# Layer 0: the FFN gate's adaLN projection moves from TensorE (attention) to VectorE (up projection)

## The chip, the cores and the metric

One Trainium2 chip (trn2), one core. The metric is device microseconds of one execution; lower is better. The kernel before was run three times: 1411.06, 1406.48 and 1403.56 us, median 1406.48 us.

## The reference, cut to what matters

Two layers of a decoder trunk on 512 tokens of width 1024, all in float32. In each layer six modulation rows of 1024 come from one product of the condition vector with `w_ada`; two of them, `g1` and `g2`, are gates on the output of the mixer and of the FFN:

```
cond = jax.nn.silu(c)
for l in range(DEPTH):
    mod = cond @ w_ada[l] + b_ada[l]
    sh1, sc1, g1, sh2, sc2, g2 = [m[:, None, :] for m in jnp.split(mod, 6, axis=-1)]
    h = x * (1 + sc1) + sh1
    y = hybrid_mixer(h, ...)                     # gMLP, retention, sparse attention, w_out
    x = layer_norm(DN_ALPHA * x + g1 * y, ln1_g[l], ln1_b[l])
    h = x * (1 + sc2) + sh2
    y = conv_ffn(h, w_up[l], conv_w[l], conv_b[l], w_down[l])
    x = layer_norm(DN_ALPHA * x + g2 * y, ln2_g[l], ln2_b[l])
```

So `g1` (columns 2048 to 3071 of `w_ada`) is needed after the output projection, and `g2` (columns 5120 to 6143) only after the down projection.

## The kernel before

**Stages.** Each layer runs its projections, then an attention stage, the output projection `w_out`, the up projection with its convolution, and the down projection. Large float32 products are split into three matmuls of a high and a low part (`mm3`, L449 to L451); ScalarE makes the high part of each weight tile (L125, `whi`) and VectorE, or GpSimd for the retention weights and `w_out`, the low part (L127, `wlo`). `Weights` (L92 to L160) walks one list of jobs in program order: loads go to SP's queue into three `wraw` buffers, and two jobs ahead are split into three `whi` and three `wlo` buffers.

**Where `w_ada` is multiplied.** `ADA_RUNS` puts the six rows into three banks of two runs of 1024 columns; bank 2 holds the gates, run 0 `g1` and run 1 `g2`.
- Layer 0, banks 1 and 2, are done by TensorE in the attention stage (`ada_bank`, L318): for each of 8 k and each run, one raw 512 KB tile is loaded through the job list and two matmuls (L327) multiply it, each giving 32 columns of the array to 512 columns of output. Here such a pair is called a group; each bank has 16. The profile records each of these float32 matmuls twice, so that a group is x4 in a row.
- Layer 1, all three banks, are done ahead by VectorE during layer 0's up projection (`ada_dve`, L332): each run loads eight 512 KB tiles on GpSimd's queue (L341) into four `araw` buffers and sums them into one `acc` tile (L343 once, then L345 seven times); then TensorE adds the 128 partitions up with matmuls by ones (L349, one group for each run), VectorE adds the bias (`ada_finish`, L363).

**Order of the work.** A scheduler sets the order within each engine from the program's order. In the attention stage `attention()` steps beside `filler()`: at each event of attention one step of the retention mixer (projections, then four chunks with L906, L917, L926, L932, L935) and, in `ADA_AT` steps, one group of L327. In the up projection, a loop over 22 column tiles `ct`, each `ct` is followed by three steps of `ada_ahead`. A step is one load and one accumulation, or the closing matmuls, or the bias.

**The gate's row.** `gate_row` (L1144) broadcasts a gate from `modg` into a `grow` tile with eight small DMAs on SP's queue (L1150). For the FFN it is called ahead of the `ct` loop.

Of the kernel before, what the change touches and what calls it, by code (L numbers as in the profile page):

```python
# [10 lines left out]
F32 = mybir.dt.float32  # L11
# [3 lines left out]
OP = mybir.AluOpType  # L15
AX = mybir.AxisListType

P = 128
# [3 lines left out]
KD = D // P  # L22
# [126 lines left out]
def tile_trunk(ctx, tc, I, tab, out, layers=L):  # L149
    nc = tc.nc  # L150
    V, A, G, T = nc.vector, nc.scalar, nc.gpsimd, nc.tensor
# [12 lines left out]
    def m4(name):  # L164
        return pool.tile([P, 1024], F32, tag="m4", name=name, bufs=5)
# [45 lines left out]

    ADA_RUNS = {0: (0, D), 1: (3 * D, 4 * D), 2: (2 * D, 5 * D)}


    WO_EARLY = 1
    WO_ORDER = ([(cc, h) for h in range(2) for cc in range(WO_EARLY)] +
# [5 lines left out]
    def ada_jobs(l, bank):  # L222
        wa = I["w_ada"][l].rearrange("(p k) n -> p k n", k=KD)
        return [(("ada", l, bank, k, h), "raw", [(lambda t: t[:, :D], wa[:, k, c0:c0 + D])])
                for k in range(KD) for h, c0 in enumerate(ADA_RUNS[bank])] + [None, None]

    def job_tm(key, l, parts):
        for h in range(2):
# [8 lines left out]
    for l in range(layers):  # L237
# [52 lines left out]
    ident = tabv("ident")  # L290
# [27 lines left out]
    def ada_bank(l, bank):  # L318

        pm = ps()  # L320
        bt = ada_bias(l, bank)
        for k in range(KD):
            for h in range(2):
                raw = ws.next(("ada", l, bank, k, h))
                for a2 in range(2):
                    a = 2 * h + a2
                    T.matmul(pm[32 * a:32 * a + 32, :], ce[:, k:k + 1].to_broadcast([P, 32]), raw[:, a2 * 512:(a2 + 1) * 512],  # L327
                             start=(k == 0), stop=(k == KD - 1), tile_position=(0, 32 * a))
                yield
        yield from ada_finish(l, bank, pm, bt)  # L330

    def ada_dve(l, bank):  # L332

        accs = []
        bt = ada_bias(l, bank)
        for c0 in ADA_RUNS[bank]:
            acc = m4("acc")
            accs.append(acc)
            for k in range(KD):
                raw = big("araw")[:, :D]  # L340
                nc.gpsimd.dma_start(raw, I["w_ada"][l].rearrange("(p k) n -> p k n", k=KD)[:, k, c0:c0 + D])  # L341
                if k == 0:
                    pin(V.tensor_scalar(acc, raw, ce[:, 0:1], None, op0=OP.mult))  # L343
                else:
                    V.scalar_tensor_tensor(acc, raw, ce[:, k:k + 1], acc, op0=OP.mult, op1=OP.add)  # L345
                yield
        pm = ps()
        for a in range(4):
            T.matmul(pm[32 * a:32 * a + 32, :], ones, accs[a // 2][:, (a % 2) * 512:(a % 2 + 1) * 512],  # L349
                     start=True, stop=True, tile_position=(0, 32 * a))  # L350
        yield
        yield from ada_finish(l, bank, pm, bt)

    def ada_bias(l, bank):
        bt = pool.tile([P, 512], F32, tag="adab", name="adab", bufs=1)
        for a in range(4):
            c0 = ADA_RUNS[bank][a // 2] + 512 * (a % 2)
            nc.gpsimd.dma_start(bt[32 * a:32 * a + 32, :], I["b_ada"][l][None, c0:c0 + 512].to_broadcast([32, 512]))
        return bt

    def ada_finish(l, bank, pm, bt):
        ms = pool.tile([P, 512], F32, tag="modg", name="modg", bufs=1) if bank == 2 else bt
        V.tensor_tensor(ms, pm, bt, op=OP.add)  # L363
        res = ms
        yield
        if bank != 2:

            pc = ps()
            for j in range(4):
                T.transpose(pc[:, j * P:(j + 1) * P], ms[:, j * P:(j + 1) * P], ident)  # L370
            res = pool.tile([P, 2, KD], F32, tag="modc", name="modc", bufs=3)
            V.tensor_copy(res.rearrange("p s (a j) -> p (s a) j", j=4),
                          pc.rearrange("p (j s x) -> p s j x", j=4, s=4)[:, :, :, 0])
            V.tensor_scalar(res[:, 1, :], res[:, 1, :], 1.0, None, op0=OP.add)
        ada_out[l, bank] = res
        yield

# [5 lines left out]
    GAINS_AT = 16  # L383

    def ada_ahead(l):
        for bank in range(3):
            yield from ada_dve(l, bank)

# [127 lines left out]
    for l in range(layers):  # L516
# [741 lines left out]
        run(to_h(NT - 1, X[NT - 1], ab, h2h, h2l))  # L1258
        first.append(up_mm(1, 0, at=pin))
        up_ps = {ct: up_mm(ct, 1, first[ct])[1] for ct in range(2)}  # L1260
        gr = gate_row(l, 2)
        for ct in range(NFF):
            if ct == GAINS_AT - 2:
                n_up = norm_rows(l, "ln1_g", "ln1_b", ALPHA)
# [14 lines left out]
            A.activation(ts_[0], ts_[0], AF.Silu)  # L1279
            V.tensor_tensor(gsl(ct), ts_[0], ts_[1], op=OP.mult)  # L1280
            for _ in range(3):
                next(ahead, None)
        run(ahead)
        lgr, lbr = norm_rows(l, "ln2_g", "ln2_b", ALPHA if l + 1 < layers else 1.0)
        if l + 1 < layers:
# [133 lines left out]
```

## Time and profile before

| | |
|---|---|
| median of three runs | 1406.48 us (1403.56 to 1411.06) |
| the profiled execution: its own time, its span | 1405.42 us, 1403.5 us |
| TensorE busy, share of the span | 96% |
| VectorE, ScalarE, GpSimd busy | 62%, 39%, 15% |
| mean granted TensorE clock | 0.99 of full speed |
| DMA | 168.91 MB, 120 GB/s on average |

The busy share of TensorE counts matmuls that overlap in the pipeline; starts of consecutive matmuls tell the pace. A wait is given in brackets with what ended it. Layer 0's attention lies between about 120 and 305 us, its `w_out` up to about 346 us, its up projection up to about 601 us and its down projection up to about 727 us.

### The profile page before, as it was taken

The numbers are of one execution on the slowest core, as the hardware profiler recorded it, in microseconds if no ns is written. First come the engines' busy times: TensorE is split into PE (matmuls) and PEld (weight loads), VectorE is DVE, ScalarE is ACT, GpSimd is POOL, SyncE is SP. The second block draws the span as 40 slices with busy tenths as digits, with TensorE's granted clock in tenths as the row PEclk, the third lists the DMA queues.
The fourth block names the chain that finished last, engine by engine and source line by source line (L and its number), as shares of the span: only waits on it lengthen the run. The fifth ranks groups of instructions, "written<-read, shape, count | busy, mean of one in ns | idle before, by whom it ended". The sixth has DMA issues, their size and how long they took to land.

```text
span 1403.5 us, 19590 instructions
## 1 busy us (share of the span) xinstructions
PE 1348.3 (96%) x7723; PEld 1108.5 (79%) x7723; DVE 872.4 (62%) x1422; ACT 549.2 (39%) x999; POOL 209.6 (15%) x206
## 2 busy tenths in 40 slices
PE   5999999899999999999989999999999999999995
PEld 4898675679978788778878987876998888888884
DVE  6767533847797787743477578475675555763337
ACT  3525334543533343332323354465253334333320
POOL 0311220325011120000000024112400000000005
PEclk9999999999999999999999999999999999999998
DMA  9832545413586674322532231111223334332221
GB/s 299 231 89 71 177 145 180 127 61 102 168 285 213 215 260 137 121 94 91 159 68 66 61 96 46 46 46 39 82 76 97 100 90 134 92 124 102 90 75 60
DMA packets 181896, 168.91 MB, mean 120 GB/s; under 512 B 23540, under 2 KB 161644, under 8 KB 181804
## 3 DMA queue, kind: packets, MB, share of 16 engines
q1 hardware_dynamic: 174252, 141.18, 33.0%
q0 software_dynamic: 7552, 26.48, 5.5%
q8 instruction: 61, 1.00, 0.3%
q14 instruction: 31, 0.25, 0.1%
HBM read 163.44 MB, written 2.10 MB: 118 GB/s over the span
## 4 chain that ended last, share of the span: by engine, by line
PE 83%; DVE 8%; ACT 3%; DMA 3%; POOL 1%; issue 1%; SPq 1%; DVEq 0%; ACTq 0%
PE ps L449 19%; PE ps L451 19%; PE ps L450 19%; PE ps L542 4%; PE ps L543 4%; PE ps L544 4%; PE ps L1028 3%; PE ps L327 2%; PE ps L1020 2%; PE ps L969 1%; PE ps L970 1%; DVE t L1170 1%; POOL xa L1171 1%; DVE pt L989 1%; DMA wraw<-in_w_up_dram 1%
## 5 line engine op out<-in xcount | busy, mean ns | idle before, releaser
L125 ACT CAST whi<-wraw 128x1024 fp32r<-128x1024 f32 (+3 forms) x187 | 185.6, 997 | 400.1 <-PE ps L450 229.5
L127 DVE TENSOR_TENSOR wlo<-wraw,whi 128x1024 fp32r<-128x1024 f32 (+3 forms) x161 | 186.4, 1162 | 168.7 <-ACT whi L125 168.3
L451 PE MATMUL ps<-h2h,wlo 128*128 128x512 f32 (+1 forms) x736 | 278.2, 378 | 0.0
L450 PE MATMUL ps<-h2l,whi 128*128 128x512 f32 (+1 forms) x736 | 277.2, 377 | 0.0
L449 PE MATMUL ps<-h2h,whi 128*128 128x512 f32 (+1 forms) x736 | 276.9, 377 | 0.0
L450 PEld LDWEIGHTS ps<-h2l,whi 128*128 128x128 f32 x736 | 138.2, 188 | 28.7 <-issue 1.7
L449 PEld LDWEIGHTS ps<-h2h,whi 128*128 128x128 f32 x736 | 138.1, 188 | 28.4 <-ACT whi L125 2.5
L451 PEld LDWEIGHTS ps<-h2h,wlo 128*128 128x128 f32 x736 | 138.3, 188 | 26.1 <-issue 0.8
L542 PE MATMUL ps<-whi,hh 128*128 128x256 f32 (+1 forms) x448 | 131.9, 294 | 0.0
L543 PE MATMUL ps<-wlo,hh 128*128 128x256 f32 (+1 forms) x448 | 128.9, 288 | 0.0
L544 PE MATMUL ps<-whi,hl 128*128 128x256 f32 (+1 forms) x448 | 127.3, 284 | 0.0
L450 PE MATMUL ps<-wlo,pt 128*128 128x512 f32 x288 | 113.9, 396 | 0.0
L449 PE MATMUL ps<-whi,pt 128*128 128x512 f32 x288 | 113.9, 396 | 0.0
L451 PE MATMUL ps<-whi,pt 128*128 128x512 f32 x288 | 111.8, 396 | 0.0
L542 PEld LDWEIGHTS ps<-whi,hh 128*128 128x128 f32 x448 | 85.4, 191 | 13.9 <-issue 11.3
L543 PEld LDWEIGHTS ps<-wlo,hh 128*128 128x128 f32 x448 | 85.5, 191 | 5.5 <-issue 5.2
L127 POOL TENSOR_TENSOR wlo<-wraw,whi 128x1024 fp32r<-128x1024 f32 x26 | 64.1, 2467 | 157.1 <-ACT whi L125 142.1
L544 PEld LDWEIGHTS ps<-whi,hl 128*128 128x128 f32 x448 | 85.4, 191 | 0.2 <-issue 0.2
L1171 POOL TENSOR_TENSOR xa<-xa,t 128x256 f32<-128x256 f32 (+1 forms) x24 | 26.8, 1121 | 368.0 <-DVE t L1170 368.0
L187 DVE TENSOR_TENSOR pt<-g,pt 128x512 fp32r<-128x512 f32 x32 | 22.1, 691 | 81.5 <-PE ps L450 79.9
L985 ACT ACTIVATE pt<-ps,sm 128x256 f32<-128x256 f32 (+2 forms) x96 | 55.7, 590 | 39.3 <-DVE sm L982 27.1
L1021 ACT COPY pT<-ps 128x128 f32<-128x128 f32 (+3 forms) x128 | 50.3, 436 | 46.8 <-PE ps L1020 46.2
(279 smaller groups left out, 2610.6 us busy)
## 6 DMA issues: line engine op xcount, KB each, us to landing
wraw<-in_w_up_dram SPq DMA_DIRECT2D x88, 512.0 KB, 3.8
araw<-in_w_ada_dram POOLq DMA_DIRECT2D x48, 512.0 KB, 5.1
wraw<-in_w_down_dram SPq DMA_DIRECT2D x44, 512.0 KB, 3.4
wraw<-in_w_ada_dram SPq DMA_DIRECT2D x32, 512.0 KB, 4.5
wraw<-in_w_in_dram SPq DMA_DIRECT2D x30, 512.0 KB, 3.9
wraw<-in_w_out_dram SPq DMA_DIRECT2D x16, 512.0 KB, 4.6
a<-in_w_ada_dram SPq DMA_DIRECT2D x14, 512.0 KB, 7.4
wraw<-in_w_in_dram SPq DMA_DIRECT2D x8, 384.0 KB, 8.3
```

The costliest lines, as they stand in the source:

```text
L125: self.nc.scalar.copy(f(hi), src)
L127: eng.tensor_tensor(f(lo), src, f(hi).bitcast(F32), op=OP.subtract)
L449: at(T.matmul(o, lh, rh, start=first, stop=False))
L450: T.matmul(o, lh, rl, start=False, stop=False)
L451: T.matmul(o, ll, rh, start=False, stop=last)
L542: T.matmul(o, a, wh[:, k - k0, :], start=(first and k == 0), stop=False)
L543: T.matmul(o, a, wl[:, k - k0, :], start=False, stop=False)
L544: T.matmul(o, b, wh[:, k - k0, :], start=False, stop=(last and k == KD - 1))
L985: A.activation(pp[e][:, :n], o[e], AF.Exp, bias=sm[:, 0, e:e + 1], accum_out=sm[:, 1, e:e + 1])
L1021: A.copy(PT[e][:, i:i + 3 * i + 1:3, :], pb[:, :(i + 1) * P].rearrange("p (j q) -> p j q", q=P))
L1028: T.matmul(po[64 * e:64 * e + 64, j * P:], VS[:, b, j, 64 * g:64 * g + 64], PT[e][:, 4 * j:4 * j + NT - j, :].rearrange("p a q -> p (a q)" ...
L1171: i = eng.tensor_tensor(X[t][:, c0:c0 + n], X[t][:, c0:c0 + n], tmp, op=OP.add)
```

## The change

Layer 0's run 1 of bank 2 (`g2`) is taken out of the job list and out of `ada_bank`, and becomes the first thing that `ada_ahead(1)` does in layer 0's up projection, by `ada_dve`. `ada_finish` writes its half of the `modg` tile. `gate_row` for the FFN is called when that is done (the step `"gate"`), no longer ahead of the loop. Layer 1 is as before.

```diff
+    ADA_PE = {1: 2, 2: 1}
 ...
     def ada_jobs(l, bank):
-                for k in range(KD) for h, c0 in enumerate(ADA_RUNS[bank])] + [None, None]
+                for k in range(KD) for h, c0 in enumerate(ADA_RUNS[bank][:ADA_PE[bank]])] + [None, None]
 ...
     def ada_bank(l, bank):
+        hs = range(ADA_PE[bank])
         for k in range(KD):
-            for h in range(2):
+            for h in hs:
                 raw = ws.next(("ada", l, bank, k, h))
...
-    def ada_dve(l, bank):
+    def ada_dve(l, bank, hs=range(2)):
+        for h in hs:
+            c0 = ADA_RUNS[bank][h]
+            acc = accs[h] = m4("acc")
...
         pm = ps()
-        for a in range(4):
-            T.matmul(pm[32 * a:32 * a + 32, :], ones, accs[a // 2][:, (a % 2) * 512:(a % 2 + 1) * 512],
-                     start=True, stop=True, tile_position=(0, 32 * a))
+        for h in hs:
+            for a in (2 * h, 2 * h + 1):
+                T.matmul(pm[32 * a:32 * a + 32, :], ones, accs[h][:, (a % 2) * 512:(a % 2 + 1) * 512],
+                         start=True, stop=True, tile_position=(0, 32 * a))
...
+        if bank == 2:
+            if (l, 2) not in ada_out:
+                ada_out[l, 2] = pool.tile([P, 512], F32, tag="modg", name="modg", bufs=1)
+            r = slice(64 * hs[0], 64 * hs[-1] + 64)
+            V.tensor_tensor(ada_out[l, 2][r], pm[r], bt[r], op=OP.add)
...
     def ada_ahead(l):
+        if l == 1:
+            yield from ada_dve(0, 2, range(1, 2))
+            yield "gate"
         for bank in range(3):
             yield from ada_dve(l, bank)
...
-        gr = gate_row(l, 2)
+        if l:
+            gr = gate_row(l, 2)
...
             for _ in range(3):
-                next(ahead, None)
+                if next(ahead, None) == "gate":
+                    gr = gate_row(l, 2)
```

In the changed kernel the lines have moved: L327 is L330, L343 is L346, L345 is L348, L349 is L353, L363 is L371 for a bank of gates, L449 to L451 are L462 to L464, L1150 is L1163, L1276, L1277 and L1280 are L1290, L1291 and L1294; in the attention stage 13 is added to a line.

The built programs show where the instructions stand. First TensorE in the retention chunks of layer 0's attention; `t` are transposed queries and keys or scores of a chunk, `vb` its values, `pT` attention weights. Before:

```order
L327 MATMUL ps<-wraw,ce 32x512 x2
L917 MATMUL ps<-t_2366 128x128 x4
L926 MATMUL ps<-vb,rot 64x64 x4
L327 MATMUL ps<-wraw,ce 32x512 x4
L932 MATMUL ps<-vb,t_2380 128x64
L935 MATMUL ps<-state,t_2366 128x64
L1020 MATMUL ps<-tb,pt 128x128 x6
```

And in the changed kernel:

```order
L930 MATMUL ps<-t_2366 128x128 x4
L939 MATMUL ps<-vb,rot 64x64 x4
L945 MATMUL ps<-vb,t_2376 128x64
L948 MATMUL ps<-state,t_2366 128x64
L1033 MATMUL ps<-tb,pt 128x128 x6
```

The chunk's matmuls now follow each other with no group of L327 between them. In all, bank 2 keeps eight of its sixteen groups, at the first eight places; one that stood in two halves now stands in one, and six places (of 1, 3, 1, 2 and 1 groups, and that half) are empty.

Second, TensorE in the up projection, between column tile 2 and column tile 3 (`h2h`, `h2l` are the two parts of the FFN's input). Before:

```order
L449 MATMUL ps<-h2h_2981,whi 128x512
L450 MATMUL ps<-h2l_2983,whi 128x512
L451 MATMUL ps<-h2h_2981,wlo 128x512
L449 MATMUL ps<-h2h_2980,whi 128x512
L450 MATMUL ps<-h2l_2982,whi 128x512
```

And in the changed kernel:

```order
L462 MATMUL ps<-h2h_2947,whi 128x512
L463 MATMUL ps<-h2l_2949,whi 128x512
L464 MATMUL ps<-h2h_2947,wlo 128x512
L353 MATMUL ps<-acc,ones 32x512 x2
L462 MATMUL ps<-h2h_2946,whi 128x512
```

The closing group of the new sum stands right behind column tile 2. The next such matmuls (L349 before) stand behind column tile 5, which is 144 matmuls of L449 to L451 further on. In the changed kernel the closing matmuls of layer 1's banks 1 and 0 stand as two groups side by side, behind column tiles 9 and 15; before, four matmuls or more of the up projection stood between the two groups of each.

Third, VectorE at the same point (`g` is a finished column tile, here tile 2, and `t` its two halves in the convolution). Before:

```order
L1276 SCALAR_TENSOR_TENSOR t_3895<-ps,pcol,t_3895 128x511
L345 SCALAR_TENSOR_TENSOR acc<-araw,ce,acc 128x1024
L1277 SCALAR_TENSOR_TENSOR t_3895<-ps,pcol,t_3895 128x510
L345 SCALAR_TENSOR_TENSOR acc<-araw,ce,acc 128x1024
L1280 TENSOR_TENSOR g_3528<-t_3891,t_3895 128x512
L127 TENSOR_TENSOR wlo<-wraw,whi 128x1024
```

And in the changed kernel:

```order
L1290 SCALAR_TENSOR_TENSOR t_3850<-ps,pcol,t_3850 128x511
L348 SCALAR_TENSOR_TENSOR acc<-araw,ce,acc 128x1024
L1291 SCALAR_TENSOR_TENSOR t_3850<-ps,pcol,t_3850 128x510
L348 SCALAR_TENSOR_TENSOR acc<-araw,ce,acc 128x1024
L1294 TENSOR_TENSOR g_3494<-t_3846,t_3850 128x512
L348 SCALAR_TENSOR_TENSOR acc<-araw,ce,acc 128x1024
L371 TENSOR_TENSOR modg<-ps,adab 64x512
L346 TENSOR_SCALAR acc<-araw,ce 128x1024
L348 SCALAR_TENSOR_TENSOR acc<-araw,ce,acc 128x1024 x4
L127 TENSOR_TENSOR wlo<-wraw,whi 128x1024
```

Ahead of these rows VectorE's order is the same in both. The third L348 shown is the eighth and last accumulation of the new sum; it stands behind the convolution of column tile 2, and the bias of the gate right behind it.

## Rows read from the trace of the kernel before

**Rows 1.** The page, part 4: shares of the chain that ended last.
```profile
PE 83%; DVE 8%; ACT 3%; DMA 3%; POOL 1%; issue 1%; SPq 1%; DVEq 0%; ACTq 0%
```
**Rows 2.** Stretches: length, busy us of each engine (instructions), clock, DMA share, GB/s.
```profile
230.00:250.00 20.00, 20.00 (x149) 11.08 (x148) 8.40 (x26) 7.76 (x20) 0.00 (x0) 1.00 0.67 219
250.00:262.00 12.00, 10.47 (x76) 6.85 (x74) 10.01 (x14) 5.78 (x11) 9.08 (x7) 1.00 0.63 203
262.00:300.00 38.00, 34.02 (x240) 26.55 (x238) 29.78 (x70) 25.18 (x73) 8.47 (x6) 1.00 0.12 37
360.00:400.00 40.00, 40.00 (x228) 34.95 (x227) 34.34 (x40) 19.06 (x24) 5.90 (x11) 1.00 0.65 205
```
**Rows 3.** Timeline of TensorE in the attention: start, duration, engine, line, operation.
```profile
137.54 0.28 PE L972 MATMUL ps<-cmaskb,identb 128*128 128x256 bf16 x1
137.75 1.05 PE L327 MATMUL ps<-wraw,ce 128*32 128x512 f32 x4
138.74 0.39 PE L542 MATMUL ps<-whi,hh 128*128 128x256 f32 x1
138.96 0.28 PE L543 MATMUL ps<-wlo,hh 128*128 128x256 f32 x1
...
245.41 1.40 PE L327 MATMUL ps<-wraw,ce 128*32 128x512 f32 x8
246.74 0.43 PE L932 MATMUL ps<-vb,t 128*128 128x64 f32 x2
```
**Rows 4.** The chain in order of time, 200 to 400 us: start, length, what.
```profile
217.42 0.97 PE ps L327 x2
...
238.51 1.84 PE ps L327 x12
...
243.46 0.98 PE ps L327 x4
```
**Rows 5.** Timeline of ScalarE, behind the last groups of bank 2.
```profile
251.77 1.05 ACT L125 CAST whi<-wraw 128x1024 fp32r<-128x1024 f32 x1 [2.65 <-DMA wraw<-in_w_out_dram]
```
**Rows 6.** Timeline of VectorE: one operation beside GpSimd's L127, and later alone.
```profile
257.99 4.58 DVE L470 TENSOR_TENSOR rot<-rot,nst 128x512 f32<-128x512 f32 x1
...
275.64 0.68 DVE L470 TENSOR_TENSOR rot<-rot,nst 128x512 f32<-128x512 f32 x1
```
**Rows 7.** Timeline of TensorE in the up projection: tile 3 begins; closing groups.
```profile
382.72 0.39 PE L449 MATMUL ps<-h2h,whi 128*128 128x512 f32 x1
...
415.45 0.40 PE L451 MATMUL ps<-h2h,wlo 128*128 128x512 f32 x1
415.77 1.05 PE L349 MATMUL ps<-acc,ones 128*32 128x512 f32 x4
416.76 0.50 PE L449 MATMUL ps<-h2h,whi 128*128 128x512 f32 x1
417.09 0.39 PE L450 MATMUL ps<-h2l,whi 128*128 128x512 f32 x1
```
**Rows 8.** Timeline of VectorE in the up projection, column tile 2, and a later L345.
```profile
386.07 0.73 DVE L1276 SCALAR_TENSOR_TENSOR t<-ps,pcol,t 128x511 f32<-128x511 f32 x1
...
389.78 0.68 DVE L1280 TENSOR_TENSOR g<-t,t 128x512 f32<-128x512 f32 x1
390.38 1.21 DVE L127 TENSOR_TENSOR wlo<-wraw,whi 128x1024 fp32r<-128x1024 f32 x1
...
392.18 1.27 DVE L345 SCALAR_TENSOR_TENSOR acc<-araw,ce,acc 128x1024 f32<-128x1024 f32 x1
410.59 1.28 DVE L345 SCALAR_TENSOR_TENSOR acc<-araw,ce,acc 128x1024 f32<-128x1024 f32 x1
```
**Rows 9.** Timeline of ScalarE at the end of column tile 2.
```profile
383.65 0.77 ACT L1275 ACTIVATE t<-ps,pcol 128x512 f32<-128x512 f32 x1
```
**Rows 10.** The tile araw: its loads on GpSimd's queue.
```profile
DMA to landing us min/median/max: 3.7/5.1/10.1
```
**Rows 11.** Timeline of TensorE between the layers.
```profile
731.86 1.94 PE L434 MATMUL ps<-tb,xa 128*128 128x128 f32 x8 [4.69 <-DVE xa L1183]
```
**Rows 12.** Stretches between the layers, columns as in rows 2.
```profile
732.00:734.00 2.00, 2.00 (x10) 2.00 (x11) 0.44 (x2) 1.43 (x3) 0.00 (x0) 0.50 0.00 0
734.00:736.00 2.00, 2.00 (x16) 2.00 (x15) 1.83 (x3) 0.11 (x1) 0.00 (x0) 0.76 0.00 0
```

More of the change, by code (lines that the diff above doesn't have):

```diff
@@ L320, in ada_bank @@
         pm = ps()
-        bt = ada_bias(l, bank)
+        hs = range(ADA_PE[bank])
+        bt = ada_bias(l, bank, hs)
         for k in range(KD):
-            for h in range(2):
+            for h in hs:
                 raw = ws.next(("ada", l, bank, k, h))
@@ L329, in ada_bank @@
                 yield
-        yield from ada_finish(l, bank, pm, bt)
-    def ada_dve(l, bank):
[L334 to L338, printed above, removed]
+        yield from ada_finish(l, bank, pm, bt, hs)
+    def ada_dve(l, bank, hs=range(2)):
+        accs = {}
+        bt = ada_bias(l, bank, hs)
+        for h in hs:
+            c0 = ADA_RUNS[bank][h]
+            acc = accs[h] = m4("acc")
             for k in range(KD):
@@ L347, in ada_dve @@
         pm = ps()
-        for a in range(4):
-            T.matmul(pm[32 * a:32 * a + 32, :], ones, accs[a // 2][:, (a % 2) * 512:(a % 2 + 1) * 512],
-                     start=True, stop=True, tile_position=(0, 32 * a))
+        for h in hs:
+            for a in (2 * h, 2 * h + 1):
+                T.matmul(pm[32 * a:32 * a + 32, :], ones, accs[h][:, (a % 2) * 512:(a % 2 + 1) * 512],
+                         start=True, stop=True, tile_position=(0, 32 * a))
         yield
-        yield from ada_finish(l, bank, pm, bt)
@@ L354, in ada_bias @@
-    def ada_bias(l, bank):
+        yield from ada_finish(l, bank, pm, bt, hs)
+    def ada_bias(l, bank, hs):
         bt = pool.tile([P, 512], F32, tag="adab", name="adab", bufs=1)
-        for a in range(4):
-            c0 = ADA_RUNS[bank][a // 2] + 512 * (a % 2)
-            nc.gpsimd.dma_start(bt[32 * a:32 * a + 32, :], I["b_ada"][l][None, c0:c0 + 512].to_broadcast([32, 512]))
-        return bt
-    def ada_finish(l, bank, pm, bt):
-        ms = pool.tile([P, 512], F32, tag="modg", name="modg", bufs=1) if bank == 2 else bt
+        for h in hs:
+            for a in (2 * h, 2 * h + 1):
+                c0 = ADA_RUNS[bank][h] + 512 * (a % 2)
+                nc.gpsimd.dma_start(bt[32 * a:32 * a + 32, :], I["b_ada"][l][None, c0:c0 + 512].to_broadcast([32, 512]))
+        return bt
@@ L363, in ada_finish @@
+    def ada_finish(l, bank, pm, bt, hs):
+        if bank == 2:
[3 more added lines that the diff above has]
+            V.tensor_tensor(ada_out[l, 2][r], pm[r], bt[r], op=OP.add)
+            yield
+            return
+        ms = bt
         V.tensor_tensor(ms, pm, bt, op=OP.add)
-        res = ms
         yield
[L366 to L374, printed above, removed]
+        pc = ps()
+        for j in range(4):
+            T.transpose(pc[:, j * P:(j + 1) * P], ms[:, j * P:(j + 1) * P], ident)
+        res = pool.tile([P, 2, KD], F32, tag="modc", name="modc", bufs=3)
+        V.tensor_copy(res.rearrange("p s (a j) -> p (s a) j", j=4),
+                      pc.rearrange("p (j s x) -> p s j x", j=4, s=4)[:, :, :, 0])
+        V.tensor_scalar(res[:, 1, :], res[:, 1, :], 1.0, None, op0=OP.add)
```

## Prediction

> **What bounds the kernel now.** I read the chain of waits on the page first: 83% of it is TensorE and 8% VectorE [rows 1]. So a microsecond on TensorE counts unless it lies beside a wait, and the question is what the change does to TensorE's order in the two stages that it touches. I read the stretches of those two stages next [rows 2]. In the retention core of the attention TensorE is busy 20.00 of 20 us from 230 to 250, has 1.53 us of idle time in 250 to 262 and 3.98 us in 262 to 300, where no group is left. In the up projection it is busy 40.00 of 40 us from 360 to 400, with VectorE at 34.34. Then I read TensorE's timeline around single groups [rows 3, 7] and the chain in order of time, on which groups of bank 2 stand as links of their own [rows 4]: there they are on the path, not beside it. Last I read who delivers what the new closing group needs: VectorE's and ScalarE's timelines around column tile 2 [rows 8, 9] and the loads of `araw` [rows 10].
>
> **What leaves the attention.** Eight of bank 2's sixteen groups go. A group alone takes 0.97 to 0.98 us [rows 4]; two side by side take 1.33 us (245.41 to 246.74 [rows 3]), three 1.84 us [rows 4]. By the order, the places emptied held a half-moved group (0.97), 1, 3, 1, 2 and 1 groups: 0.97 + 0.98 + 1.84 + 0.98 + 1.33 + 0.98 = 7.08 us. Around a group the neighbours start later, too: the matmul ahead of one takes 0.21 us to the next start (137.54 to 137.75) and the one behind 0.22 us (138.74 to 138.96 [rows 3]), with 256 columns each; the 512 columns of the up projection start every 0.23 us ((415.77 - 382.72) / 144 [rows 7]), so 256 take half, 0.12. That is 0.1 us on either side, 0.2 us for a place, 1.2 us for six. Together **-8.3 us**.
>
> All six places lie after 217 us, in the retention core, where ScalarE and VectorE prepare each chunk's operands, and a group there may also fill time that would be a wait. How much, the trace of before does not show, so I bound it. At best the 1.53 + 3.98 = 5.5 us of idle time [rows 2] goes as well, since the loads of `w_out` come earlier: ScalarE waits 2.65 us for the first of them behind the `w_ada` loads [rows 5], and VectorE's L470 takes 4.58 us there against 0.68 us later [rows 6], beside GpSimd's L127. At worst everything taken out after 230 us comes back as waits: 0.98 + 1.84 + 0.98 + 1.33 + 0.98 = +6.1 us. I take 0: the stretch without groups loses 3.98 of 38 us, 10% [rows 2]; the same share of the 14.9 us that are left of 230 to 250 is 1.5 us, and the 1.53 us of idle time in 250 to 262 is about what the earlier `w_out` loads give back.
>
> **What TensorE gains in the up projection.** One closing group for `g2`: 0.99 us (415.77 to 416.76) and 0.1 us on either side (415.45 to 415.77 and 416.76 to 417.09, against 0.23 [rows 7]), 1.2 us. Against that the closing groups of banks 1 and 0 now stand side by side: 1.33 + 0.2 instead of 2 x 1.2, 0.87 us less for each bank. Net **-0.5 us**.
>
> **The wait that this group brings.** The group stands behind column tile 2, and TensorE works in order. In before's time it reaches the place at 382.72 us, when tile 3 begins [rows 7]. The group needs the eighth accumulation. On VectorE this stands behind tile 2's convolution: two halves of L1276's kind, two accumulations between, the product L1280. Tile 2's own matmuls have only just ended when TensorE gets there. ScalarE's last step on them begins at 383.65 and takes 0.77 us [rows 9], VectorE's L1276 begins at 386.07, and L1280 ends at 390.46; the operation behind it starts at 390.38 [rows 8]. In the changed kernel that operation is the eighth accumulation, 1.27 us [rows 8]: it ends at 391.65. So TensorE stands still for 391.65 - 382.72 = **+8.9 us**. It has nothing else to do, because tile 3 is queued behind the group, and no idle time follows that could absorb it: 40.00 of 40 us are busy [rows 2]. Below: if VectorE took tile 2 up as soon as ScalarE is done (384.42) and needed 390.46 - 386.07 = 4.4 us and 1.27 us more, 390.1, or 7.4 us of wait. Above: a load of `araw` lands in 5.1 us at the median and 10.1 us at most [rows 10]; if the eighth is such a one, 5.0 us more, 13.9. I take 8.9, since the tile's convolution is what VectorE has ahead of it in either case.
>
> **The clock behind that wait.** Between the layers TensorE idles 4.69 us [rows 11], and the granted clock of the next two stretches of 2 us is 0.50 and 0.76 [rows 12], where 0.50 is the lower level, 1.2 of 2.4 GHz. At 0.50 a stretch does half its work, so this costs 2 x 0.5 + 2 x 0.24 = 1.5 us. The new wait is twice as long, and I take the same **+1.5 us** (0 if the clock holds, 3 if it stays down twice as long).
>
> The rule that speaks against the first term is in the Trainium skill, page TensorEngine Tiling (Array Packing), section Key Properties: tiles operate independently, different tiles can load weights and multiply in parallel. The trace agrees with it for groups side by side, which take 1.33 us and not twice 0.98 [rows 3, 4]; of a lone group it shows the contrary, so I keep 7.1 us; by the rule the term would be 4.3 us smaller and the sum 1412.3, as rival 3 works out from rows.
>
> **What I cost at nothing.** VectorE's eight accumulations are at most 8 x 1.27 = 10.2 us more work [rows 8] in a stage where it has 40 - 34.34 = 5.66 us free in each 40 [rows 2], and the stage is some 250 us long: cover of some 35 us. That they delay other VectorE work (behind the bias stand five accumulations, at most 6.4 us, before L127 splits the next weight tile) is covered by the weights split ahead: three column tiles are 144 matmuls, so one of its two weight tiles is 24, 24 x 0.23 = 5.5 us, and two are split ahead, 11 us. If that cover were gone, 6.4 us would be lost once. The 16 `w_ada` loads of layer 1's bank 1 queue on GpSimd behind the bias of `g2`; they delay accumulations whose closing groups stand behind tiles 9 and 15 with room. Bank 2's last sums end nearer to the down projection; their late end costs nothing until layer 1 asks for them. The eight loads of 512 KB change queue, not number: in the attention they leave a DMA share of 0.67, in the up projection they join one of 0.65 [rows 2]. The eight `grow` loads wait on SP's queue for the gate; weight loads queued behind them are late by less than one wait of TensorE's, in which nothing is consumed. The row itself is only read behind the down projection.
>
> **The sum.** -8.3 + 0 - 0.5 + 8.9 + 1.5 = +1.6 us. The profiled execution took 1405.42 us, so the changed one takes 1407.0. This execution lies 1.06 us under the median of 1406.48, so I give **1408 us** for the median. A measurement of this kernel can tell some 0.5%, 7 us, from no change: faster is below 1399.4, slower above 1413.5. The forecast is no change: what the attention gives, the wait takes.
>
> **The rivals.**
> 1. *No wait at the new group* (chance 0.08). The closing group of bank 1 in before did not wait: TensorE reached it at 415.77 us, and the last accumulation of this kind had ended at 410.59 + 1.28 = 411.87 [rows 7, 8], 3.9 us earlier. If VectorE ran a column tile ahead like that, the change would keep its gain: 1408 - 8.9 - 1.5 = 1397.6 us. Against it stands VectorE's order: the eighth sum is behind the convolution of the very tile whose matmuls TensorE has just ended.
> 2. *The groups were cover* (chance 0.11, slower). The chunk's matmuls now follow each other directly, and each needs what ScalarE and VectorE make from the one before. If that chain is longer in a chunk than the matmuls that are left, from 230 us on the removed 6.1 us turn into waits: 1408 + 6.1 = 1414.1 us. It decides from the point where TensorE, now 20.00 of 20 busy [rows 2], has less work in these 20 than the chain: 20 - (0.98 + 1.84 + 0.98 + 1.33) = 14.9 us are left. For it: 3.98 us idle right behind, where no group stands [rows 2]. Against it: those groups are links of the chain [rows 4].
> 3. *A group shares the array* (chance 0.03). If the two halves of a group, and neighbouring groups, ran beside each other throughout, a removed group would be worth only what a second one adds, 1.33 - 0.98 = 0.35 us [rows 3, 4]: 8 x 0.35 = 2.8 instead of 7.1 us, so +4.3 and 1412.3 us. Against it: a lone group occupies its 0.98 us by itself, from the start of one neighbour to the next [rows 3]; only groups side by side gain.
>
> That the change does not do what it says is ruled out by the order: the eight groups are gone from the attention's rows.
>
> **How the numbers follow.** The forecast has 0.78; its own range is 1400 to 1415: at the low end the idle time and the clock's price go (-5.5 - 1.5 = -7.0, 1401), at the high end either the whole cover (+6.1) or a late load with a clock that stays down longer (+5.0 + 1.5) comes, not both. Of its 0.78, 0.03 is faster, 0.70 the same, 0.05 slower. Rival 1 is faster by 0.08; rival 2 gives 0.08 slower and 0.03 the same, being near the bound; rival 3 is the same. Together faster 0.11, same 0.76, slower 0.13. Rivals 2 and 3 lie in the range and rival 1 just below, so 1400 to 1415 leaves out less than 2 in 10.
>
> **What would show it.** In the changed kernel's attention: no links of groups in the chain from 231 us on, and the output projection beginning some 8 us earlier. In the up projection: an idle time of some 9 us ahead of the first closing group, ended by VectorE's accumulation, and 0.5 of clock right behind it. If there is no such wait, rival 1 holds; if new waits stand in the retention chunks and the output projection begins no earlier, rival 2; if it begins only some 3 to 4 us earlier with no new waits, rival 3. If the wait is much longer than 9 us and ended by a DMA, my bound on the load was wrong.

## The result and the profile after

The changed kernel took 1415.24 us (median of 11 runs, 1409.40 to 1418.86), the kernel before 1406.22 us (11 runs). The ratio is **1.0056, 95% interval 1.0042 to 1.0069**: slower by 0.56%, where 1408 us and "no change" had been forecast. Taken by the ratio, that is 1406.48 x 1.0056 = 1414.4 us, just within the range of 1400 to 1415; the median itself lies 0.24 us above it. The profiled execution is the fastest of the eleven: 1409.40 us, span 1407.6 us, mean granted clock 0.987.

TensorE's share of the chain fell from 83% [rows 1] to 80%, on page part 4 of the changed kernel:

```profile
PE 80%; DVE 9%; DMA 3%; ACT 3%; issue 2%; POOL 2%; SPq 1%; DVEq 0%; ACTq 0%; POOLq 0%
```

**The attention is shorter, as forecast.** TensorE's first matmul of the output projection starts at 268.84 us instead of 278.42, although the attention itself starts 1.0 us later (124.26 against 123.25); so the stage is 10.6 us shorter. These are the stretches that answer to those of rows 2 (length, busy us of PE, PEld, DVE, ACT, POOL with their instructions, clock, DMA share, GB/s):

```profile
230.00:250.00 20.00, 19.28 (x165) 13.94 (x163) 15.00 (x43) 13.21 (x31) 8.17 (x5) 1.00 0.47 139
250.00:262.00 12.00, 12.00 (x93) 9.64 (x92) 8.39 (x21) 7.60 (x27) 1.93 (x2) 1.00 0.20 46
262.00:300.00 38.00, 34.73 (x236) 25.70 (x235) 20.76 (x47) 22.52 (x54) 10.42 (x5) 1.00 0.14 42
360.00:400.00 40.00, 31.28 (x149) 24.82 (x148) 31.79 (x36) 14.06 (x18) 9.05 (x17) 0.91 0.80 242
```

In 230 to 300 us the idle time is 0.72 + 0 + 3.27 = 4.0 us; before it was 0 + 1.53 + 3.98 = 5.5 [rows 2]. Between the two first matmuls TensorE is idle for 2.2 us, against 4.0 us before. In this execution nothing came back as a wait.

**The new wait is there.** The last row already shows it: TensorE, busy 40.00 of 40 us before, is idle for 8.72. Its timeline around column tile 2 (start, duration, engine, line, operation, and the wait with its end):

```profile
375.24 0.40 PE L464 MATMUL ps<-h2h,wlo 128*128 128x512 f32 x1
384.36 1.92 PE L353 MATMUL ps<-acc,ones 128*32 128x512 f32 x4 [8.72 <-DVE acc L348]
386.21 0.80 PE L462 MATMUL ps<-h2h,whi 128*128 128x512 f32 x1
386.80 0.63 PE L463 MATMUL ps<-h2l,whi 128*128 128x512 f32 x1
```

And VectorE's, which answers to rows 8. The order is that of the prediction: convolution, product, and only then the eighth accumulation, ending at 384.30:

```profile
380.57 0.74 DVE L1291 SCALAR_TENSOR_TENSOR t<-ps,pcol,t 128x510 f32<-128x510 f32 x1
381.23 1.27 DVE L348 SCALAR_TENSOR_TENSOR acc<-araw,ce,acc 128x1024 f32<-128x1024 f32 x1
382.42 0.69 DVE L1294 TENSOR_TENSOR g<-t,t 128x512 f32<-128x512 f32 x1
383.02 1.28 DVE L348 SCALAR_TENSOR_TENSOR acc<-araw,ce,acc 128x1024 f32<-128x1024 f32 x1
386.33 0.69 DVE L371 TENSOR_TENSOR modg<-ps,adab 64x512 f32<-64x512 f32 x1 [2.03 <-PE ps L353]
```

**The clock falls in the wait and stays down behind it.** Stretches of the changed kernel, columns as above:

```profile
380.00:382.00 2.00, 0.00 (x0) 0.00 (x0) 2.00 (x3) 0.00 (x0) 0.53 (x1) 0.71 0.83 263
382.00:384.00 2.00, 0.00 (x0) 0.00 (x0) 2.00 (x3) 0.62 (x1) 0.53 (x1) 0.50 0.94 282
384.00:386.00 2.00, 1.64 (x4) 0.19 (x4) 0.30 (x1) 0.00 (x0) 0.53 (x1) 0.50 0.84 272
386.00:388.00 2.00, 2.00 (x7) 1.46 (x6) 1.61 (x3) 0.00 (x0) 0.69 (x2) 0.58 0.81 291
388.00:390.00 2.00, 2.00 (x11) 1.63 (x10) 1.96 (x2) 0.00 (x0) 2.00 (x5) 1.00 0.73 219
```

From the moment TensorE works again, 1.64 x 0.50 + 2 x 0.42 = 1.7 us are lost. The closing group takes 1.92 us instead of 0.98.

**A second fall of the clock was not forecast.** It stands at the start of the up projection, where TensorE waits for the normalised tokens in both kernels. The changed kernel there:

```profile
338.00:340.00 2.00, 1.56 (x13) 1.57 (x14) 2.00 (x6) 0.00 (x0) 1.54 (x3) 0.97 1.06 378
340.00:342.00 2.00, 2.00 (x11) 2.00 (x11) 1.69 (x6) 1.51 (x4) 0.40 (x2) 0.50 1.08 404
342.00:344.00 2.00, 2.00 (x14) 2.00 (x14) 1.57 (x3) 1.21 (x3) 0.39 (x1) 0.68 1.00 401
```

The kernel before, at the same point of its program:

```profile
346.00:348.00 2.00, 0.60 (x6) 0.47 (x5) 1.87 (x5) 0.72 (x2) 2.00 (x3) 1.00 0.86 245
348.00:350.00 2.00, 2.00 (x19) 2.00 (x18) 2.00 (x7) 0.57 (x2) 0.64 (x2) 1.00 1.06 377
```

TensorE had been idle for 1.85 us in the one and 1.40 us in the other; only the first lost (0.03 + 0.50 + 0.32) x 2 = 1.7 us to the clock.

**What else the up projection waits for.** The waits of TensorE from 350 to 620 us in the changed kernel (line, what ended it, us in total, times, longest):

```profile
PE ps L353 <- DVE acc L348: 8.7, 1, 8.7
PE ps L380 <- DVE adab L375: 1.8, 1, 1.8
PE ps L419 <- issue: 1.7, 1, 1.7
```

Before, the only one was 1.1 us ahead of L406 (now L419). The 1.8 us are new, at 466.8 us: the transposes of the first layer 1 sum wait for its bias on VectorE. This is bank 0, with which the loop of `ada_ahead` begins; what the prediction says of bank 1's loads and first closing group holds for bank 0.

**The ledger of the profiled executions.** TensorE's first matmul of each stage, and the last of all, in us:

| | before | after | after - before |
|---|---|---|---|
| attention (first L972, now L985) | 123.25 | 124.26 | +1.0 |
| output projection | 278.42 | 268.84 | -9.6 |
| up projection | 348.39 | 339.28 | -9.1 |
| down projection | 600.86 | 603.73 | +2.9 |
| last matmul | 1387.62 | 1391.08 | +3.5 |

The up projection became 12.0 us longer and ate the gain. From the profiled executions the change costs 3.5 to 4.0 us, by the medians 9.0. A part of the rest shows in the clock that each run lists. Span x (1 - mean clock) is the time at full clock that a run misses, idle or not: 21.6 us on average over the eleven runs, 1407.6 x 0.013 = 18.3 in the profiled one. For the kernel before it is 15.7 us over 28 runs (15.3 to 16.4 in the four sets of runs with the experiments), 1403.5 x 0.010 = 14.0 in the profiled one. So the profiled executions differ by 4.3 us of clock and the averages by 5.9: the clock explains some 1.6 of the 5 us by which the medians differ more, and the rest is open. The changed kernel's profile shows its best execution, and what the others lose cannot be read from it. (Some 6 to 7 us of the missing clock lie at the very end, where TensorE has no work left, in every profile.)

### The profile page after: what moved, and what is told of

Its sections match the earlier page's. It is cut to its first block, busy times and chain, and to the rows that moved or that the text cites. A ratio compares the mean times of both kernels' runs of the same rounds, so it can differ in the third digit from the quotient of the medians.

```text
span 1407.6 us, 19547 instructions
## 1 busy us (share of the span) xinstructions
PE 1340.4 (95%) x7695; PEld 1108.0 (79%) x7695; DVE 877.2 (62%) x1431; ACT 549.1 (39%) x999; POOL 214.1 (15%) x214
## 4 chain that ended last, share of the span: by engine, by line
PE 80%; DVE 9%; DMA 3%; ACT 3%; issue 2%; POOL 2%; SPq 1%; DVEq 0%; ACTq 0%; POOLq 0%
PE ps L463 18%; PE ps L462 18%; PE ps L464 18%; PE ps L555 4%; PE ps L556 4%; PE ps L557 4%; PE ps L1041 3%; PE ps L1033 2%; PE ps L330 2%; DMA a<-in_w_ada_dram 1%; PE ps L982 1%; PE ps L983 1%; DVE t L1183 1%; POOL xa L1184 1%; DMA wraw<-in_w_up_dram 1%
## 5 line engine op out<-in xcount | busy, mean ns | idle before, releaser
L127 DVE TENSOR_TENSOR wlo<-wraw,whi 128x1024 fp32r<-128x1024 f32 (+3 forms) x161 | 186.8, 1165 | 167.1 <-ACT whi L125 166.8
L464 PE MATMUL ps<-h2h,wlo 128*128 128x512 f32 (+1 forms) x736 | 278.9, 379 | 0.0
L462 PE MATMUL ps<-h2h,whi 128*128 128x512 f32 (+1 forms) x736 | 277.5, 377 | 0.0
L462 PEld LDWEIGHTS ps<-h2h,whi 128*128 128x128 f32 x736 | 139.1, 189 | 29.1 <-issue 1.7
L464 PEld LDWEIGHTS ps<-h2h,wlo 128*128 128x128 f32 x736 | 139.2, 189 | 25.1
L462 PE MATMUL ps<-whi,pt 128*128 128x512 f32 x288 | 113.0, 396 | 0.0
L464 PE MATMUL ps<-whi,pt 128*128 128x512 f32 x288 | 110.7, 396 | 0.0
L127 POOL TENSOR_TENSOR wlo<-wraw,whi 128x1024 fp32r<-128x1024 f32 x26 | 64.1, 2468 | 137.3 <-ACT whi L125 121.9
L348 DVE SCALAR_TENSOR_TENSOR acc<-araw,ce,acc 128x1024 f32<-128x1024 f32 x49 | 62.6, 1277 | 13.3 <-DMA araw<-in_w_ada_dram 13.2
```

The lines of the kernel that those rows point to most:

```text
L127: eng.tensor_tensor(f(lo), src, f(hi).bitcast(F32), op=OP.subtract)
L462: at(T.matmul(o, lh, rh, start=first, stop=False))
L464: T.matmul(o, ll, rh, start=False, stop=last)
```

## Experiments

Five timed rounds each, beside the kernel before on the same chip, except for before_again. "Missing clock" is the figure just explained, averaged over the runs.

| kernel | ratio to before | 95% interval | missing clock, us |
|---|---|---|---|
| the change | 1.0056 | 1.0042 to 1.0069 | 21.6 |
| att_only | 0.9961 | 0.9945 to 0.9976 | 17.7 |
| up_only | 1.0087 | 1.0064 to 1.0110 | 21.8 |
| close_3 | 0.9990 | 0.9971 to 1.0010 | 19.4 |
| g2_third | 0.9993 | 0.9979 to 1.0007 | 19.9 |
| fill_wait | 1.0036 | 1.0014 to 1.0057 | 18.2 |
| no_idle | 0.9977 | 0.9963 to 0.9991 | 14.5 |
| before_no_idle | 0.9987 | 0.9974 to 1.0000 | 11.8 |
| wo_dve | 0.9976 | 0.9962 to 0.9991 | 17.4 |
| wo_dve_no_idle | 0.9971 | 0.9959 to 0.9983 | 12.6 |
| spread_groups | 0.9959 | 0.9944 to 0.9974 | 15.8 |
| spread_no_idle | 0.9959 | 0.9946 to 0.9971 | 14.0 |

### One half of the change at a time: att_only and up_only

att_only takes the groups out of the attention and sums `g2` nowhere. Layer 0's FFN takes `g1`'s row as its gate instead, so the kernel leaves `g2` out and only its time is of use:

```diff
         if l == 1:
-            yield from ada_dve(0, 2, range(1, 2))
-            yield "gate"
...
-        if l:
-            gr = gate_row(l, 2)
+        gr = gate_row(l, 2 if l else 0)
```

> The change's part in the attention alone: the eight groups are gone, and the sum of g2 is left out of the up projection (the FFN of layer 0 takes g1's row as its gate, so that the row is fetched as before). Theory (attention and wait are two separate terms): the attention gives the 10.6 us that the changed kernel's profile shows up to the output projection, so about 1396 us, ratio 0.993, and no idle time behind column tile 2. Rival (the groups were cover, their time comes back as waits): 1402 to 1406. Third possibility: the clock falls at the start of the up projection as it did in the changed kernel's profile (0.50 and 0.68 around 341 us), then 1398, and the 5 us by which the changed kernel's median lies above its profiled run may come from there: up to 1401.

up_only leaves all sixteen groups in the attention and sums `g2` a second time in the up projection, with loads of its own:

```diff
-    ADA_PE = {1: 2, 2: 1}
+    ADA_PE = {1: 2, 2: 2}
```

> The change's part in the up projection alone: the attention multiplies all sixteen groups of bank 2 as before, and g2 is summed a second time by VectorE and closed behind column tile 2. Theory: the wait of some 9 us, some 2 us of low clock and the closing group of 1.2 us, less 1.7 us for the pairs: 1406 + 10 to 12 = 1416 to 1418, ratio 1.007 to 1.009. Rival (there is no separate wait; the changed kernel lost its time in the attention): 1406 to 1408. Third possibility: the load on the DMA queues and on VectorE costs more than the one wait: over 1420.

Measured: att_only 1401.83 us, 0.9961, a gain of 0.39% or 5.5 us (3.4 to 7.7). That is half of the 10.6 us which the stage was shorter in the changed kernel's profile. The theory's 0.993 is missed: by the ratio the time is 1400.8 us, inside the third possibility, and the median itself lies between that and the rival's 1402. up_only 1420.43 us, 1.0087, a loss of 12.2 us (9.0 to 15.5), in the theory's range by the ratio, though the median by itself is just over 1420. The wait stands in it again, with the clock at 0.50 up to 398 us:

```profile
391.98 1.92 PE L353 MATMUL ps<-acc,ones 128*32 128x512 f32 x4 [8.82 <-DVE acc L348]
```

So the change is the sum of two halves, -0.39% + 0.87% = +0.48%, against +0.56% measured. The half with the wait went as expected; the half in the attention gave less. att_only's profile shows a reason. TensorE waits 2.4 us in the retention chunks, at 241.5 us, where the changed kernel's profile has a wait of 0.7 us:

```profile
PE ps L942 <- ACT pt L995: 2.4, 1, 2.4
```

Behind it the clock is 0.54 and 0.61 for two stretches of 2 us.

### The closing group behind another tile: close_3 and g2_third

```diff
+        if l == 0:
+            for _ in range(1):
+                yield
         pm = ps()
```

> The changed kernel with one empty step between the eighth accumulation of g2 and its closing group, by which the group stands behind column tile 3 and no longer behind tile 2. Theory: TensorE gets there 11 us later, when the accumulation has ended, so no wait and no low clock: 1415 - 8.7 - 2 = 1404 us, about 0.998 of the kernel before. Rival (the wait only moves to the next thing that VectorE owes, such as the split of the weights): 1413 to 1415 with an idle time elsewhere in the up projection.

g2_third moves the sum instead:

```diff
-        if l == 1:
-            yield from ada_dve(0, 2, range(1, 2))
-            yield "gate"
         for bank in range(3):
+            if l == 1 and bank == 2:
+                yield from ada_dve(0, 2, range(1, 2))
+                yield "gate"
             yield from ada_dve(l, bank)
```

> The changed kernel with the sum of g2 behind layer 1's banks 0 and 1 and ahead of bank 2, so that its closing group stands behind column tile 15 and the first closing groups behind tile 5, as before. Theory: no wait as in the kernel before, 1400 to 1404 us, 0.996 to 0.998. Rival (any closing group that follows eight accumulations waits): an idle time of 5 us or more ahead of it, 1408 or more.

Measured: 0.9990 and 0.9993. Against the changed kernel's 1.0056 one empty step is worth 0.66%, 9.3 us, about what the wait and the clock behind it were put at (8.9 + 1.5). The waits of close_3 from 350 to 620 us hold no trace of it; L356 is the closing groups' line there:

```profile
PE ps L422 <- DMA t<-in_c_pos_v_dram: 1.7, 1, 1.7
PE ps L356 <- DVE acc L348: 0.5, 1, 0.5
PE ps L465 <- DVE pcol L426: 0.3, 1, 0.3
```

g2_third's time is 0.9993, within the theory's 0.996 to 0.998 only at the interval's end. It has a wait of 1.6 us ahead of a closing group near the end of the stage. Neither kernel beats the kernel before beyond its interval, as the attention's gain without the wait should have let it: 0.39% was there in att_only, 0.1% is left. Of these 4 us the traces name 1.2 for the closing group and about 1 for such small waits. By the table the two kernels also miss 1.7 and 2.2 us more clock than att_only; how much of that lies in idle time, which costs nothing, stays open. close_3's profile cannot tell: it shows one of its better executions, 1402.39 us against a median of 1406.83, with a wait of only 0.7 us in the retention chunks.

### Work in place of the wait: fill_wait

```diff
         pm = ps()
+        if l == 0:
+            for i in range(36):
+                T.matmul(pm, fillh[0][0][:, 0, :128], fillh[0][1][:, 0, :], start=True, stop=True)
...
+        fillh[:] = [(h2h[0], h2h[1])]
```

> The changed kernel with 36 matmuls of 128x512 behind column tile 2 (36 x 0.23 = 8.3 us of work whose result is thrown away), and the closing group of g2 half a column tile later: TensorE works through the time that was the wait. Theory (the wait costs its 8.7 us and, behind it, some 2 us of low clock): no stretch of low clock between 375 and 400 us, and some 2 us less than the changed kernel: ratio 1.003 to 1.005. Rival (the clock's part is nothing): the same as the changed kernel, 1.0056.

Measured: 1.0036 (1.0014 to 1.0057). TensorE is busy all through the place, and the clock holds:

```profile
376.00:380.00 4.00, 4.00 (x19) 3.30 (x18) 4.00 (x5) 2.05 (x3) 0.53 (x1) 1.00 0.72 201
380.00:384.00 4.00, 4.00 (x20) 3.27 (x19) 4.00 (x5) 2.36 (x3) 1.05 (x2) 1.00 0.95 306
384.00:388.00 4.00, 4.00 (x19) 3.34 (x18) 4.00 (x6) 0.00 (x0) 0.53 (x1) 1.00 0.90 270
```

So the idle time, and not the work around it, brings this fall of the clock. The time lies where the theory put it, 0.2% or 2.8 us under the change, but its interval just takes in 1.0056 too. The trace decides here, not the time.

### Work in the other idle times: no_idle, before_no_idle and before_again

```diff
+    NW = (7, 18, 9)
...
+    def warm(n, a, b):
+        pw = ps()
+        for _ in range(n):
+            pin(T.matmul(pw, a, b, start=True, stop=True))
...
+                    if l == 0 and b == 2:
+                        warm(NW[0], yh[0][:, 0, :128], yh[0][:, 0, :])
...
```

Likewise 18 and 9 such matmuls stand ahead of two groups of transposes between the layers. no_idle is this on close_3, before_no_idle on the kernel before.

> The kernel close_3 with matmuls whose result is thrown away in three idle times of TensorE: 7 ahead of the transposes at the start of the up projection (1.6 us in a gap of 1.96), 18 and 9 between the layers (4.1 us in 4.69, 2.1 us in 2.1 to 2.9). Theory (a part of what the shorter attention gave is lost again to the clock, at the start of the up projection and between the layers): the granted clock is 1.00 at these three places, where the four kernels with the shorter attention showed 0.50 at the first, and the time falls by 2 to 5 us against close_3: 1402 to 1405 us, ratio 0.996 to 0.998. Rival (the clock falls whatever TensorE does there): ratio 0.999 to 1.001 as close_3.

> The kernel before with the same thrown-away matmuls in the same three idle times: the control for no_idle. Theory: in the kernel before the clock did not fall at the start of the up projection, so only the fall between the layers goes (1.6 us or so): ratio 0.998 to 1.000, and no_idle lies 2 to 5 us below it. Rival (no_idle's gain has nothing to do with the shorter attention): both gain the same, and the distance between them is that of close_3 to the kernel before, 0 to 2 us.

> The kernel before, unchanged, for a second profile of it. If the clock at the start of the up projection (346 to 350 us) is 1.00 again and the attention begins near 123 us, the falls of the clock seen there in the four kernels with the shorter attention belong to them; if it falls here too, they are chance and can't be put down to the change.

Measured: 0.9977 and 0.9987; missing clock 14.5 us against close_3's 19.4, and 11.8 against 16.4 of the kernel before in that comparison. In both profiles the clock is 1.00 at all three places. The control gains as much as the kernel under test (0.13%, 1.8 us, each), so its rival holds as to time. Neither gain is clear of the noise. My 2 to 5 us between the two are not borne out: it is 0.1%, no more than lay between close_3 and the kernel before. So the clock's fall at the start of the up projection is seen in the traces, but no time shows that it costs close_3 its 1.7 us; the intervals are too wide to exclude it.

before_again answers the other question. It took 1406.08 us, TensorE waited 1.72 us at the start of the up projection, and the clock stayed up:

```profile
346.00:348.00 2.00, 1.43 (x13) 1.43 (x14) 2.00 (x5) 0.00 (x0) 1.68 (x3) 1.00 1.04 357
348.00:350.00 2.00, 2.00 (x20) 2.00 (x19) 1.83 (x7) 1.37 (x4) 0.26 (x2) 1.00 1.07 325
```

Over all profiles without matmuls put in there: the clock fell at this point in all seven with eight groups (idle time 1.85 to 1.97 us) and in none of the three with sixteen (before, before_again, up_only; 1.40 to 1.72 us). So the fall goes with the shorter attention. Whether the few tenths of idle time decide it or the moment at which it comes, no run here separates. The later start of the attention in the changed kernel's profile is chance: before_again starts it at 125.29 us.

### What the groups had covered: wo_dve, wo_dve_no_idle and spread_groups

Of the first six profiles with eight groups four (att_only, g2_third, fill_wait, no_idle) show a wait of 2.3 to 3.8 us in the retention chunks, and two (the changed kernel, close_3) one of 0.7 us. In the four profiles with sixteen groups no wait ahead of a chunk's matmuls is over 1.1 us. In no_idle's profile the wait in the retention chunks is 3.8 us:

```profile
PE ps L955 <- DVE t L943: 3.8, 1, 3.8
```

It waits behind this VectorE operation, which scales a softmax,

```profile
232.65 6.45 DVE L1012 TENSOR_SCALAR pt<-pt,sm,gates 128x384 f32<-128x384 f32 x2
```

beside GpSimd's low parts of the output projection's first weights:

```profile
230.88 2.37 POOL L127 TENSOR_TENSOR wlo<-wraw,whi 128x1024 fp32r<-128x1024 f32 x1 [24.49 <-ACT whi L125]
233.19 1.01 POOL L368 DMA_DIRECT2D adab<-in_b_ada_dram  x2
234.21 4.66 POOL L127 TENSOR_TENSOR wlo<-wraw,whi 128x1024 fp32r<-128x1024 f32 x2
```

In the changed kernel's own profile the same operation falls between two of GpSimd's, which end at 233.59 and begin again at 234.70, and takes 0.87 us:

```profile
233.59 0.87 DVE L1002 TENSOR_SCALAR pt<-pt,sm,gates 128x384 f32<-128x384 f32 x2
```

In att_only's the scaling gets away with 1.21 us, and another VectorE operation is caught, a subtraction that takes 0.69 us in no_idle's profile; the wait of 2.4 us stands behind it (g2_third has the same with 3.45 us):

```profile
232.69 2.36 POOL L127 TENSOR_TENSOR wlo<-wraw,whi 128x1024 fp32r<-128x1024 f32 x1 [24.32 <-ACT whi L125]
234.47 1.21 DVE L999 TENSOR_SCALAR pt<-pt,sm,gates 128x384 f32<-128x384 f32 x2
237.00 4.69 POOL L127 TENSOR_TENSOR wlo<-wraw,whi 128x1024 fp32r<-128x1024 f32 x2
238.71 3.54 DVE L187 TENSOR_TENSOR yl<-yc,yh 128x512 fp32r<-128x512 f32 x1
```

The Trainium skill, page SBUF — State Buffer, section SBUF: two separate sides, says that VectorE, in its modes with two ports or with two inputs in SBUF, and GpSimd share a pair of ports which the one that starts first holds for its whole instruction, while the other is blocked. The rows agree in part. The long operations end just behind GpSimd's, at 239.10 us against 238.87 and at 242.25 against 241.69. But the second half of no_idle's scaling is recorded from 233.38 us on, ahead of GpSimd's operation at 234.21, and still ended behind it, so the recorded start does not tell who is blocked.

wo_dve gives these three low parts to VectorE, in close_3:

```diff
-            eng = self.nc.gpsimd if key[0] in self.on_pool else self.nc.vector
+            early = key in (("wo", 0, 0, 0), ("wo", 0, 0, 1), ("wo", 0, 1, 0))
+            eng = self.nc.gpsimd if key[0] in self.on_pool and not early else self.nc.vector
```

> The kernel close_3 with the low parts of the first three weight tiles of layer 0's output projection made by VectorE and no longer by GpSimd. In four of the six profiles with the shorter attention TensorE waits 2.3 to 3.8 us around 235 to 245 us, in the profile of no_idle for a VectorE operation (softmax scaling, 2 x) that takes 6.45 us beside GpSimd's three low parts and 0.87 us in the changed kernel's profile, where it does not meet them. Theory (a part of what the removal gave comes back as this wait, and the clock falls behind it): no wait over 1 us there, VectorE's operation under 1 us, and the time 1 to 4 us under close_3, ratio 0.996 to 0.998. Rival (the wait is one that any order has, and VectorE's own low parts take its place): 0.999 to 1.001 with a wait there again.

> wo_dve and no_idle together, as the candidate that should beat both kernels. Theory (the two gains are of different places): 1401 to 1404 us, ratio 0.994 to 0.997. Rival (they pay the same loss twice): 0.9977 as no_idle alone.

spread_groups leaves the low parts where they are and gives each of the eight groups every second place, so that they reach into the retention chunks again:

```diff
-                for k in range(KD) for h, c0 in enumerate(ADA_RUNS[bank][:ADA_PE[bank]])] + [None, None]
+                if h < ADA_PE[bank] else None
+                for k in range(KD) for h, c0 in enumerate(ADA_RUNS[bank])] + [None, None]
...
                 yield
+            if len(hs) == 1:
+                yield
```

> The kernel close_3 with the eight groups that TensorE keeps spread over every second place of bank 2, so that the last ones stand in the retention chunks again and the output projection's weights load later. Rival of the prediction (the removed groups were cover in the retention chunks): the wait of 2 to 4 us at 235 to 245 us is gone, and the time is 2 to 4 us under close_3, ratio 0.996 to 0.998. Theory (a group costs the same wherever it stands, and the loads of the output projection come too late again): 0.999 to 1.001, with some 1.5 us of idle time behind the last groups as in the kernel before.

Measured: wo_dve 0.9976, 0.14% under close_3 with overlapping intervals. VectorE's operation takes 0.87 us, as expected, but a wait of 1.4 us is left where "no wait over 1 us" was expected, and one of 2.3 us in wo_dve_no_idle's profile. With GpSimd out of the way VectorE's own low parts stand in the chunks, so its meeting with GpSimd is not all of the wait. Both together, wo_dve_no_idle, give 0.9971, between the theory's 0.997 and the rival's 0.9977, and decide nothing. spread_groups is the best, **0.9959**, 1399.24 us against 1404.21. In its profile GpSimd's low parts come later and one by one, and the softmax scaling between them meets none and takes 1.00 us, with 512 instead of 384 columns:

```profile
235.31 2.37 POOL L127 TENSOR_TENSOR wlo<-wraw,whi 128x1024 fp32r<-128x1024 f32 x1 [27.48 <-ACT whi L125]
239.23 1.00 POOL L369 DMA_DIRECT2D adab<-in_b_ada_dram  x2 [1.56 <-DVE modg L377]
240.25 2.36 POOL L127 TENSOR_TENSOR wlo<-wraw,whi 128x1024 fp32r<-128x1024 f32 x1
243.70 2.36 POOL L127 TENSOR_TENSOR wlo<-wraw,whi 128x1024 fp32r<-128x1024 f32 x1 [1.08 <-PE ps L925]
```

```profile
242.64 1.00 DVE L1008 TENSOR_SCALAR pt<-pt,sm,gates 128x512 f32<-128x512 f32 x2
```

TensorE's wait in the chunks is 1.3 us there. So the prediction's second rival was partly right: in the retention chunks the groups had covered something. spread_groups moves two things at once, the groups and the loads of `w_out` behind them; which of the two gives the gain was not separated. By the table it also misses 3.6 us less clock than close_3, so a part of the 4.4 us between them may be the clock and not the chunks.

### The two best together: spread_no_idle

> spread_groups with the thrown-away matmuls of no_idle in the same three idle times. Theory (the clock's falls at the start of the up projection and between the layers still cost spread_groups what they cost close_3, 0.1%): ratio 0.994 to 0.996 and a clock of 1.00 at the three places. Rival (spread_groups owes part of its gain to fewer falls of the clock, so that nothing is left to take): 0.9955 to 0.9965.

Measured: 0.9959, the same as without. The number lies in the range of both; that it does not differ from spread_groups speaks for the rival, that nothing is left to take. spread_groups beats both the kernel before (by 0.41%) and the changed kernel (by 1.0%).

## Why the prediction was right and where it was wrong

- **The terms on TensorE** held. Its busy time in the attention fell by 8.8 us in the profiled executions (from 151.17 to 142.41 us between the stage's first matmul and the output projection's, idle time left out); predicted were 8.3.
- **The wait** held: 8.72 us against 8.9, ended by the eighth accumulation, by the mechanism named. In up_only it is 8.82. One empty step ahead of the group removes it and 0.66% of time.
- **The clock behind that wait** held where it was looked for: 1.7 us against 1.5. The term as a whole, +1.5, was the step that failed in size. Over the runs the missing clock rose by 21.6 - 15.7 = 5.9 us, of which 0.29 x 2 + 0.50 x 2 = 1.6 us lie in the wait itself and cost nothing. That leaves at most some 4 us against 1.5. I had looked for falls only behind the new wait; the shorter attention brings another at the start of the up projection (1.7 us), and a third behind the retention chunks in some executions (att_only, which has only these, misses 17.7 - 15.7 = 2.0 us more than the kernel before). This third is not the shorter attention's alone: before_no_idle's profile, with sixteen groups, has one too (0.60 and 0.55 from 264 to 268 us). And behind the wait itself the clock can stay down longer: in up_only's profile to 398 us, 6 us after TensorE began again, 3 us lost.
- **The cover in the attention**, taken as 0, was the other one. "Everything removed comes back" (+6.1) was too much and "nothing" too little: att_only gained 5.5 us instead of 8.3, and four of the first six profiles with eight groups show a wait of 2.3 to 3.8 us in the chunks. How much of the 2.8 us is this wait and how much the clock was not separated. I had row 6 before me, VectorE at 4.58 us beside GpSimd's L127, and read it as a stall that the change would take away. The earlier loads only moved GpSimd's work next to other VectorE operations.
- **What was costed at nothing** held but for one thing: with the closing groups of bank 0 side by side, its transposes wait 1.8 us for VectorE's bias. That uses up the 1.7 us that the pairs were to save.
- **The forecast** of no change ended at its edge: the kernel is 0.56% slower, and the interval of the ratio, 0.42 to 0.69%, contains the bound of 0.5%. That the time still lies at the upper end of the range is partly luck: the range counted cover or a longer fall of the clock as its upper end, "not both", and a part of both came. By the time alone rival 2 with its 1414.1 us fits better; the wait of 8.72 us, the output projection that starts 9.6 us earlier and att_only's gain speak against it as the main cause. By halves, the attention gave 5.5 us where 8.3 + 0 was forecast, and the up projection cost 12.2 us where 8.9 + 1.5 - 0.5 = 9.9 was: +6.7 instead of -8.3 + 9.9 = +1.6. Both large terms of the sum were right; cover and clock beside them were each some 2 to 3 us too low, as far as the intervals tell.

## What to carry to other kernels

A small instruction that is moved onto the limiting engine costs what its producer is behind at that point, not its own duration: 1 us of matmul cost some 9 here, and one empty step took that away. Before taking filler work off the limiting engine, look at what the other two engines do to each other at that moment, since what the filler covered shows only once it is gone. And count every idle time that the change lengthens or moves as a possible fall of the clock, with its price from a fall seen elsewhere in the trace.

## What the runs showed of the hardware that was not expected

- The same VectorE operation took 0.87 us (the changed kernel), 1.21 us (att_only) or 6.45 us (no_idle) in executions of kernels with the same attention. The first began as one of GpSimd's tensor operations ended. The other two both began some 0.6 us ahead of such an end; GpSimd's next tensor operation followed 1.9 us later in att_only and 1.0 us later in no_idle, and only there was VectorE held up until GpSimd was done.
- An idle time of 1.85 to 1.97 us at the start of the up projection was followed by a clock of 0.50 in seven profiles of seven, one of 1.40 to 1.72 us in none of three; each fall took about 1.7 us or less from TensorE there. Longer idle times were not always followed by one: 2.92 us between the layers, in the profile of the kernel before, had a clock of 1.00 behind it.
